# Delta rule's inverse: blocks of 32 by substitution in two passes, in place of blocks of 16 and one more doubling

## The chip, the cores and the metric

The kernel runs on one core of a Trainium2 chip. The core has TensorE (PE, matrix products and transposes), VectorE (DVE, elementwise work and sums along a row), ScalarE (ACT, activations and copies), GpSimd (POOL) and SyncE (SP, which issues most DMAs). The metric is the device time of one execution in microseconds (us); a time given for a kernel is the median of several executions.

## The reference, cut to what matters

One layer of a decoder trunk for 256 positions: a combined projection, three branches (gated delta rule, HGRN2, attention into a memory), their gated sum, an output projection and an MLP. The change is in the gated delta rule:

```python
def gated_deltanet(q, k, v, beta, logdecay):
    # chunkwise; per head and chunk
    dec = jnp.exp(jnp.where(causal, gam[..., :, None] - gam[..., None, :], -jnp.inf))
    lower = jnp.where(strict, bc[..., :, None] * jnp.einsum('bhnid,bhnjd->bhnij', kc, kc) * dec, 0.0)
    a_mat = lower + jnp.eye(CHUNK, dtype=lower.dtype)
    rhs = jnp.concatenate([vc * bc[..., None], kc * (bc * jnp.exp(gam))[..., None]], axis=-1)
    sol = lax.linalg.triangular_solve(a_mat, rhs, left_side=True, lower=True, unit_diagonal=True)
    ...
```

The kernel uses chunks of 128 positions in place of 64 and forms the inverse of the triangular matrix itself. There are 8 heads and two chunks; four heads make a head group, so one head group has 8 matrices of 128 x 128, and there are two head groups.

## The kernel before, in words

**Weights.** Most of the work is products of activations with f32 weights. A weight group is 256 rows by 512 columns of a weight matrix, 128 partitions x 1024 numbers in SBUF, 512 KB. SP loads it (`load_w_raw`, L163, tile w, four buffers); ACT casts it to a high part wh (L174); DVE takes the difference as a low part wl (L175); wh and wl have four buffers each. TensorE then makes three products of 512 columns per row block, or in the "joined" form two products of 512 and 256 columns (L206 to L208 in `unit`, L223 and L225 in `products_joined`). A unit has 8 such groups, or 4 in a branch's second projection.

**Background work.** Everything that is no weight product is written as Python generators, put in a list and advanced by `tick`, once per weight group. `rate` says how many generator steps (yields) one tick advances; R1 to R4 are its values in four stretches: R1 for the delta rule's projections, R2 for the units of branch C (attention's output), R3 for the projections of HGRN2, R4 for the units of branch A's output. The generators are taken first in, first out; a few short ones (convolution, gates) go ahead. The framework that builds the program then fixes the order on each engine's queue from these steps, its own estimates of durations, and the buffers that are free; at run time each engine takes its queue strictly in order.

**The inverse (`gen_a`, one per head group).** U holds the strictly upper part of eight matrices. Its diagonal blocks of BL = 16 go through DRAM: eight small writes into scr, and eight loads that give every one of the 16 rows of a block the whole block (tile Lb, 16 x 16 numbers for each of 8 matrices in each partition), both issued by POOL. DVE then does back substitution on all blocks at once, one column at a time (L880 multiplies, L881 sums, 15 columns), in Xc, a row of 16 numbers for each of the 8 matrices. L884 spreads Xc over the diagonal blocks of X with the block mask mblk. TensorE transposes X into XT (L891), and then doubles the block size from 16 to 32, from 32 to 64 (each: products pw L911 and pzt L916, a masked copy into XT L918, transposes back into X L924, copies L912 and L925) and from 64 to 128 (L900, L905). Behind that come the products with the values and the head norm. Xc and Lb have one buffer; tiles of the general pool (tag g) have 25.

**Masks.** `gen_masks` makes, early in the kernel and as background work, masks of diagonal blocks and mT[s], which marks the upper off-diagonal part that a doubling from s to 2s fills.

Of the kernel before, what the change touches and what calls it, by code (L numbers as in the profile page):

```python
# [10 lines left out]
F32 = mybir.dt.float32  # L11
# [3 lines left out]
ALU = mybir.AluOpType  # L15
AX = mybir.AxisListType

P = 128
D = 2048
S = 256  # L20
NT = S // P
# [12 lines left out]
KG = 2  # L34
BL = 16
WB = 4
R1, R2, R3, R4 = 1.1, 1.0, 1.0, 1.2


@with_exitstack  # L40
def tile_trunk(ctx: ExitStack, tc, a):
    nc = tc.nc
    V, A, T, G = nc.vector, nc.scalar, nc.tensor, nc.gpsimd

    cst = ctx.enter_context(tc.tile_pool(name="cst", bufs=1))
# [3 lines left out]
    lp = ctx.enter_context(tc.tile_pool(name="lp", bufs=1))  # L49
    sp = ctx.enter_context(tc.tile_pool(name="sp", bufs=16))  # L50
    sp64 = ctx.enter_context(tc.tile_pool(name="sp64", bufs=2))
    dp = ctx.enter_context(tc.tile_pool(name="dp", bufs=2, space=bass.MemoryType.DRAM))
# [5 lines left out]
    def nm(s):  # L58
        cnt[0] += 1
        return f"{s}_{cnt[0]}"  # L60

    def g4(name, shape=(P, 1024), dt=F32):
        return gp.tile(list(shape), dt, tag="g", name=nm(name))
# [11 lines left out]
    def bank(name):  # L75
        return pbp.tile([P, 512], F32, tag="bp", name=nm(name))

    def const(name, shape, dt=F32):
        return cst.tile(list(shape), dt, tag=name, name=name)
# [11 lines left out]
    pin = tc.keep_in_program_order  # L91
# [309 lines left out]
    mgtr = const("mgtr", [P, P], F32R)  # L401
    msk2 = const("msk2", [P, 2, P])
    dblk = const("dblk", [P, BL])
    mblk = const("mblk", [P, P])
    mT = {s: const(f"mT{s}", [P, P]) for s in (1, 2, 4, 8, 16, 32, 64)}

    def gen_masks():
        G.affine_select(out=mgt, in_=ones, pattern=[[-1, P]], base=0, channel_multiplier=1,
                        compare_op=ALU.is_gt, fill=0.0)
        G.affine_select(out=mlt, in_=ones, pattern=[[1, P]], base=0, channel_multiplier=-1,  # L410
                        compare_op=ALU.is_gt, fill=0.0)
        pin(V.tensor_tensor(out=caus, in0=mlt, in1=ident, op=ALU.add))
        pin(V.tensor_copy(mgtr, mgt))
        pin(V.tensor_copy(msk2[:, 0, :], mlt))
        pin(V.tensor_scalar(out=msk2[:, 1, :], in0=caus, scalar1=-1.0, scalar2=None, op0=ALU.mult))
        pin(V.tensor_reduce(out=dblk, in_=ident.rearrange("p (k c) -> p c k", c=BL), axis=AX.X, op=ALU.add))
        yield
        prev = ident
        for s in (1, 2, 4, 8, 16, 32, 64):
            b = 2 * s  # L420
            if b < P:
                cur = mblk if b == BL else cst.tile([P, P], F32, tag=f"blk{b.bit_length() % 2}", name=f"blk{b}")
                v3 = cur.rearrange("p (n s) -> p n s", s=b)
                G.affine_select(out=v3, in_=ones.rearrange("p (n s) -> p n s", s=b),
                                pattern=[[-b, P // b], [0, b]], base=0, channel_multiplier=1,
                                compare_op=ALU.is_ge, fill=0.0)
                G.affine_select(out=v3, in_=v3, pattern=[[b, P // b], [0, b]], base=b - 1,
                                channel_multiplier=-1, compare_op=ALU.is_ge, fill=0.0)
            else:
                cur = ones  # L430
            d = cst.tile([P, P], F32, tag="mdiff", name=f"mdiff{s}")
            pin(V.tensor_tensor(out=d, in0=cur, in1=prev, op=ALU.subtract))
            pin(V.tensor_tensor(out=mT[s], in0=d, in1=mlt, op=ALU.mult))
            prev = cur
            yield

# [138 lines left out]
    for u in range(2):  # L575
        k = unit_joined(lambda kt: memB[kt // 2][:, kt % 2], w_kv, 512 * u)
# [188 lines left out]
    def gen_a(hg, kc, qc, vc, z):  # L765
# [21 lines left out]
        for t in range(NT):  # L787
            dl = g4("dl", (P, 2, 4, P), F32R)
            pd = bank("dec")
            for i, l_ in enumerate((ldh, ldl)):  # L790
                V.tensor_tensor(out=dl[:, i], in0=bc(caus, 4),
                                in1=l_.bitcast(F32)[:, t, hs].unsqueeze(2).to_broadcast([P, 4, P]), op=ALU.mult)
# [5 lines left out]
        for t in range(NT):  # L798
            V.tensor_tensor(out=d2[t], in0=dec[:, t * 4:t * 4 + 4, :].unsqueeze(2).to_broadcast([P, 4, 2, P]),
                            in1=msk2.unsqueeze(1).to_broadcast([P, 4, 2, P]), op=ALU.mult)  # L800
# [13 lines left out]
        U, AQ = g4("U", (P, 8, P)), g4("AQ", (P, 8, P))  # L814
        rck = small("rck", 8)
        for t in range(NT):
            pks = [gram(t, t, hp) for hp in range(2)]
            for h in range(4):
                jk = g4("jk", (P, P))
                V.scalar_tensor_tensor(out=jk, in0=pks[h // 2][:, (h % 2) * S:(h % 2) * S + P], scalar=1.0, in1=ident,  # L820
                                       op0=ALU.mult, op1=ALU.mult, accum_out=sse[:, t * 4 + h:t * 4 + h + 1])
            ts = slice(t * 4, t * 4 + 4)
# [3 lines left out]
                                   op0=ALU.mult, op1=ALU.mult)  # L826
# [3 lines left out]
            for h in range(4):  # L830
                b = t * 4 + h
                for w, dst in ((0, U), (1, AQ)):
                    V.scalar_tensor_tensor(out=dst[:, b, :], in0=pks[h // 2][:, (h % 2) * S + w * P:(h % 2) * S + w * P + P],
                                           scalar=cneg[:, b:b + 1], in1=d2[t][:, h, w, :],
                                           op0=ALU.mult, op1=ALU.mult)
                if h % 2 == 1:
                    yield

        NB = P // BL
        scr = dp.tile([NB, 8, BL, BL], F32, tag="scr", name=nm("scr"))  # L840
        Lb = lp.tile([P, 8, BL * BL], F32, tag="lb", name=nm("lb"))
        for k in range(NB):
            sl = slice(k * BL, (k + 1) * BL)
            pin(G.dma_start(scr[k].rearrange("b c m -> c b m"), U[sl, :, sl]))
        for k in range(NB):
            G.dma_start(Lb[k * BL:(k + 1) * BL].rearrange("p b m -> p (b m)"),
                        scr[k:k + 1].rearrange("k b c m -> k (b c m)").to_broadcast([BL, 8 * BL * BL]))
        yield
        ct0, cp0 = small("ct0", 4), small("cp0", 4)
        V.tensor_tensor(out=ct0, in0=cneg[:, 0:4], in1=t0e[:, hs], op=ALU.mult)  # L850
# [11 lines left out]
        for t in range(NT):  # L862
# [3 lines left out]
            for h in range(4):  # L866
                b = t * 4 + h
# [2 lines left out]

        X, XT, W = g4("X", (P, 8, P)), g4("XT", (P, 8, P)), g4("W", (P, 8, P))
        V.memset(W, 0.0)
        V.memset(Lb[:, :, 0:BL * BL:BL + 1], 1.0)
        Xc = lp.tile([P, 8, BL], F32, tag="xc", name=nm("xc"))
        V.tensor_copy(Xc, dblk.unsqueeze(1).to_broadcast([P, 8, BL]))
        yield
        for c in range(BL - 2, -1, -1):
            n = BL - c
            tm = lp.tile([P, 8, BL], F32, tag="tm", name=nm("tm"), bufs=2)
            V.tensor_tensor(out=tm[:, :, 0:n], in0=Xc[:, :, c:BL], in1=Lb[:, :, c * BL + c:(c + 1) * BL], op=ALU.mult)  # L880
            V.tensor_reduce(out=Xc[:, :, c], in_=tm[:, :, 0:n], axis=AX.X, op=ALU.add)  # L881
            if c % 2 == 0:
                yield
        V.tensor_tensor(out=X.rearrange("p b (k c) -> p b k c", c=BL), in0=Xc.unsqueeze(2).to_broadcast([P, 8, NB, BL]),  # L884
                        in1=mblk.rearrange("p (k c) -> p k c", c=BL).unsqueeze(1).to_broadcast([P, 8, NB, BL]), op=ALU.mult)
        yield
        yield
        for t in range(NT):
# [2 lines left out]
                T.transpose(pt[:, h * P:(h + 1) * P], X[:, t * 4 + h, :], ident)  # L891
            A.copy(XT[:, t * 4:t * 4 + 4, :], pt.rearrange("p (h i) -> p h i", h=4))
        yield
        for s in (s_ for s_ in (2, 4, 8, 16, 32, 64) if s_ >= BL):
            last = s == 64
            pw = bank("pw")
            if last:

                for b in range(8):
                    T.matmul(pw[64:128, b * 64:(b + 1) * 64], U[0:64, b, 64:128], X[0:64, b, 0:64], start=True, stop=True)  # L900
                A.copy(W[64:128, :, 0:64], pw[64:128, :].rearrange("p (b s) -> p b s", b=8))
                yield
                pzt = bank("pzt")
                for b in range(8):
                    T.matmul(pzt[0:64, b * 64:(b + 1) * 64], W[64:128, b, 0:64], XT[64:128, b, 64:128],  # L905
                             start=True, stop=True)
                A.copy(XT[0:64, :, 64:128], pzt[0:64, :].rearrange("p (b s) -> p b s", b=8))
                yield
                break
            for b in range(8):  # L910
                T.matmul(pw[:, b * 64:(b + 1) * 64], U[:, b, :], half_view(X, s, False)[:, b], start=True, stop=True)  # L911
            A.copy(half_view(W, s, False), pw.rearrange("p (b n s) -> p b n s", b=8, s=s))  # L912
            yield
            pzt = bank("pzt")
            for b in range(8):
                T.matmul(pzt[:, b * 64:(b + 1) * 64], W[:, b, :], half_view(XT, s, True)[:, b],  # L916
                         start=True, stop=True)
            V.copy_predicated(half_view(XT, s, True), half_mask(mT[s], s, True),  # L918
                              pzt.rearrange("p (b n s) -> p b n s", b=8, s=s))
            yield  # L920
            for t in range(NT):
                pt = bank("X")
                for h in range(4):
                    T.transpose(pt[:, h * P:(h + 1) * P], XT[:, t * 4 + h, :], ident)  # L924
                A.copy(X[:, t * 4:t * 4 + 4, :], pt.rearrange("p (h i) -> p h i", h=4))  # L925
            yield
# [11 lines left out]
        for h in range(4):  # L938
            V.scalar_tensor_tensor(out=r1[:, h, :], in0=pr[:, h * P:(h + 1) * P],
                                   scalar=e1e[:, hg * 4 + h:hg * 4 + h + 1], in1=nv[:, 4 + h, :],  # L940
                                   op0=ALU.mult, op1=ALU.add)
# [236 lines left out]
    for hg in range(2):  # L1178
        k, g = forget(unit_joined(hboth, w_in, OFF_BF + 512 * hg), hg)
# [216 lines left out]
    for e in range(1, NE):  # L1396
        cur = mlp_in(e)
# [20 lines left out]
```

## Time and profile before

| | |
|---|---|
| median of 3 executions | 1807.99 us (1807.24 to 1808.0) |
| the profiled execution | 1807.64 us |
| its span, first to last instruction | 1805.9 us |
| DVE, L880 and L881, both head groups | 7.0 and 6.9 us, 30 instructions each |
| TensorE, busy in that span | 1794.3 us |

The span is what the views of the trace show; the rest of an execution's time lies around it. All times in the trace are counted from the span's start. The delta rule's inverses lie at about 357 to 421 us (head group 0) and 519 to 579 us (head group 1).

### The profile page before, as it was taken

What the parts mean: (1) busy time and instruction counts of PE and PEld (TensorE: products, weight loads), DVE (VectorE), ACT (ScalarE), POOL (GpSimd) and SP (SyncE); (2) the same over time, 40 slices, a digit from 0 to 9 for tenths busy, and PEclk for the clock granted to TensorE, in tenths of its full rate; (3) what the DMA queues carried; (4) which work ended last, traced back from release to release, by engine and by line L of the source; (5) the groups of instructions that cost most, each with busy time, mean ns of one, the idle gap of its engine ahead of it and who ended that gap; (6) DMA issues with size and microseconds to landing.
All of it is one profiled execution on the core that took longest, in us unless ns stands there. A gap on an engine that the chain in (4) does not pass through costs nothing.

```text
span 1805.9 us, 23842 instructions
## 1 busy us (share of the span) xinstructions
PE 1794.3 (99%) x9241; PEld 1531.7 (85%) x9241; DVE 1133.6 (63%) x1518; ACT 909.3 (50%) x1156; POOL 42.8 (2%) x68
## 2 busy tenths in 40 slices
PE   9999999999999999999999999999999999999998
PEld 7888888888888888888888888888888888888886
DVE  6865678755764677696555557655656565655556
ACT  7645565544564565555444445544444444444433
POOL 1000000200200000000000000000000000000000
PEclk9999999999999999999999999999999999999999
DMA  8575655754665556465666675566666666666664
GB/s 273 198 199 154 187 152 150 215 174 136 175 182 162 154 167 192 140 186 175 199 186 187 211 233 163 186 188 195 190 193 191 189 218 189 192 191 191 186 197 137
DMA packets 174946, 333.40 MB, mean 185 GB/s; under 512 B 13144, under 2 KB 14832, under 8 KB 174576
## 3 DMA queue, kind: packets, MB, share of 16 engines
q1 hardware_dynamic: 169280, 325.10, 58.7%
q10 hardware_dynamic: 4528, 4.54, 0.9%
q0 software_dynamic: 1024, 2.23, 0.7%
q8 instruction: 72, 1.18, 0.3%
q14 instruction: 42, 0.34, 0.1%
HBM read 329.60 MB, written 2.23 MB: 184 GB/s over the span
## 4 chain that ended last, share of the span: by engine, by line
PE 98%; issue 0%; DMA 0%; ACT 0%; DVE 0%; POOL 0%; DVEq 0%; POOLq 0%; ACTq 0%
PE mm L223 23%; PE mm L206 18%; PE mm L208 18%; PE mm L207 18%; PE mm L225 12%; PE pa L1115 1%; PE pw L911 0%; PE pzt L916 0%; DMA lrow<-in_lb_raw 0%; PE mm L367 0%; PE mm L368 0%; PE mm L370 0%; PE idle L331 0%; PE tr L1253 0%; PE tr L356 0%
## 5 line engine op out<-in xcount | busy, mean ns | idle before, releaser
L175 DVE TENSOR_TENSOR wl<-w,wh 128x1024 fp32r<-128x1024 f32 x600 | 731.1, 1223 | 519.2 <-ACT wh L174 517.5
L174 ACT CAST wh<-w 128x1024 fp32r<-128x1024 f32 x600 | 629.8, 1052 | 710.9 <-PE mm L208 445.1
L223 PE MATMUL mm<-h2h,wh 128*128 128x512 f32 x960 | 230.4, 391 | 0.0
L206 PE MATMUL mm<-wh,hh 128*128 128x512 f32 x576 | 227.5, 395 | 0.0
L208 PE MATMUL mm<-wh,hh 128*128 128x512 f32 x576 | 224.7, 390 | 0.0
L207 PE MATMUL mm<-wl,hh 128*128 128x512 f32 x576 | 224.4, 390 | 0.0
L223 PEld LDWEIGHTS mm<-h2h,wh 128*128 128x128 f32 x960 | 176.3, 188 | 34.1
L206 PE MATMUL mm<-wh,mh 128*128 128x512 f32 x512 | 199.2, 389 | 0.0
L207 PE MATMUL mm<-wl,mh 128*128 128x512 f32 x512 | 199.2, 389 | 0.0
L208 PE MATMUL mm<-wh,ml 128*128 128x512 f32 x512 | 199.2, 389 | 0.0
L223 PE MATMUL mm<-hh,wh 128*128 128x512 f32 x768 | 192.3, 393 | 0.3 <-DVE sum L261 0.3
L223 PEld LDWEIGHTS mm<-hh,wh 128*128 128x128 f32 x768 | 138.5, 189 | 25.8 <-issue 0.5
L208 PEld LDWEIGHTS mm<-wh,hh 128*128 128x128 f32 x576 | 108.1, 188 | 22.7
L225 PEld LDWEIGHTS mm<-h2h,wl 128*128 128x128 f32 x960 | 123.1, 191 | 4.7
L206 PEld LDWEIGHTS mm<-wh,hh 128*128 128x128 f32 x576 | 108.2, 188 | 21.4
L207 PEld LDWEIGHTS mm<-wl,hh 128*128 128x128 f32 x576 | 108.3, 188 | 21.2
L225 PE MATMUL mm<-h2h,wl 128*128 128x256 f32 x960 | 124.8, 283 | 0.0
L207 PEld LDWEIGHTS mm<-wl,mh 128*128 128x128 f32 x512 | 96.1, 188 | 20.0
L208 PEld LDWEIGHTS mm<-wh,ml 128*128 128x128 f32 x512 | 96.1, 188 | 19.9
L206 PEld LDWEIGHTS mm<-wh,mh 128*128 128x128 f32 x512 | 96.1, 188 | 19.9
L225 PEld LDWEIGHTS mm<-hh,wl 128*128 128x128 f32 x768 | 102.1, 191 | 5.7
L225 PE MATMUL mm<-hh,wl 128*128 128x256 f32 x768 | 104.9, 283 | 0.0
(388 smaller groups left out, 1919.2 us busy)
## 6 DMA issues: line engine op xcount, KB each, us to landing
w<-in_w_in SPq DMA_DIRECT2D x240, 512.0 KB, 3.8
w<-in_w_mlp_in SPq DMA_DIRECT2D x128, 512.0 KB, 3.9
w<-in_w_mlp_out SPq DMA_DIRECT2D x128, 512.0 KB, 3.9
w<-in_w_out SPq DMA_DIRECT2D x32, 512.0 KB, 4.2
w<-in_w_kv_mem SPq DMA_DIRECT2D x30, 512.0 KB, 5.1
w<-in_w_br_c SPq DMA_DIRECT2D x16, 512.0 KB, 4.2
w<-in_w_br_a SPq DMA_DIRECT2D x16, 512.0 KB, 4.5
w<-in_w_br_b SPq DMA_DIRECT2D x16, 512.0 KB, 3.6
```

The lines of the kernel that those rows point to most:

```text
L174: q(A.copy(wh[:, js, 0:width], w[:, js, 0:width]))
L175: q(V.tensor_tensor(out=wl[:, js, 0:width], in0=w[:, js, 0:width], in1=wh.bitcast(F32)[:, js, 0:width], op=ALU.subtract))
L206: T.matmul(o, st, wh[:, j, :], start=kt == 0, stop=False)
L207: T.matmul(o, st, wl[:, j, :], start=False, stop=False)
L208: T.matmul(o, sl, wh[:, j, :], start=False, stop=kt == nk - 1)
L223: T.matmul(ps[c], wh[:, j, c * P:(c + 1) * P], both[j], start=k0 + j == 0, stop=end)
L225: T.matmul(ps[c][:, 0:S], wl[:, j, c * P:(c + 1) * P], both[j][:, 0:S], start=False, stop=end)
L1115: T.matmul(pas[h][:, t * 192:t * 192 + 192], kp[:, h, t * P:(t + 1) * P], qp[:, h * 2 + t, 0:192], start=True, stop=True)
```

## The change

The substitution goes to blocks of 32 without a larger Lb. Each row of X keeps two halves of 16 columns in Xc (index w). First pass (w = 1): the substitution as before, each row with its own block of 16. Then, for the rows in the second half of a block of 32, the result is carried over to the first half's columns: the off-diagonal 16 x 16 blocks of U (written to scx and loaded into two tiles Lx of the general pool) are multiplied with the row and summed (the row product). Lb's rows of the second halves are loaded again with the first halves' blocks, and a second pass (w = 0) substitutes the first half's columns. rfirst and rsecond are columns of ones and zeros that tell the rows of the first half from those of the second. mblk becomes the mask of the diagonal blocks of 32 without their upper off-diagonal part. The doubling from 16 to 32 on TensorE is left out; those from 32 and 64 stay. R2 goes from 1.0 to 1.15 and R3 from 1.0 to 1.1.

```diff
-R1, R2, R3, R4 = 1.1, 1.0, 1.0, 1.2
+R1, R2, R3, R4 = 1.1, 1.15, 1.1, 1.2
...
+            if s == BL:
+                pin(V.tensor_tensor(out=mblk, in0=cur, in1=mT[s], op=ALU.subtract))
+                pin(V.tensor_reduce(out=rfirst, in_=mT[s], axis=AX.X, op=ALU.add))
+                pin(V.tensor_scalar(out=rfirst, in0=rfirst, scalar1=1.0 / BL, scalar2=None, op0=ALU.mult))
+                pin(V.tensor_scalar(out=rsecond, in0=rfirst, scalar1=-1.0, scalar2=1.0, op0=ALU.mult, op1=ALU.add))
...
+        scx = dp.tile([NB // 2, 8, BL, BL], F32, tag="scx", name=nm("scx"))
         Lb = lp.tile([P, 8, BL * BL], F32, tag="lb", name=nm("lb"))
+        Lx = [g4("Lx", (P, 4, BL * BL)) for t in range(NT)]
+
+        def spread(rows, src):
+            G.dma_start(rows, src.rearrange("k b c m -> k (b c m)").to_broadcast([rows.shape[0], rows.shape[1]]))
+
         for k in range(NB):
             sl = slice(k * BL, (k + 1) * BL)
             pin(G.dma_start(scr[k].rearrange("b c m -> c b m"), U[sl, :, sl]))
         for k in range(NB):
-            G.dma_start(Lb[k * BL:(k + 1) * BL].rearrange("p b m -> p (b m)"),
-                        scr[k:k + 1].rearrange("k b c m -> k (b c m)").to_broadcast([BL, 8 * BL * BL]))
+            spread(Lb[k * BL:(k + 1) * BL].rearrange("p b m -> p (b m)"), scr[k:k + 1])
+        for k in range(NB // 2):
+            r0 = 2 * k * BL
+            G.dma_start(scx[k].rearrange("b c m -> c b m"), U[r0:r0 + BL, :, r0 + BL:r0 + 2 * BL])
+        for k in range(NB // 2):
+            r0 = 2 * k * BL
+            for t in range(NT):
+                spread(Lx[t][r0:r0 + 2 * BL].rearrange("p b m -> p (b m)"), scx[k:k + 1, t * 4:t * 4 + 4])
...
-        V.memset(Lb[:, :, 0:BL * BL:BL + 1], 1.0)
-        Xc = lp.tile([P, 8, BL], F32, tag="xc", name=nm("xc"))
-        V.tensor_copy(Xc, dblk.unsqueeze(1).to_broadcast([P, 8, BL]))
-        yield
-        for c in range(BL - 2, -1, -1):
...
+        Xc = lp.tile([P, 8, 2, BL], F32, tag="xc", name=nm("xc"))
+        V.tensor_copy(Xc[:, :, 1, :], dblk.unsqueeze(1).to_broadcast([P, 8, BL]))
+        yield
+
+        def substitute(w):
+            V.memset(Lb[:, :, 0:BL * BL:BL + 1], 1.0)
+            for c in range(BL - 2, -1, -1):
+                n = BL - c
+                tm = lp.tile([P, 8, BL], F32, tag="tm", name=nm("tm"), bufs=2)
+                V.tensor_tensor(out=tm[:, :, 0:n], in0=Xc[:, :, w, c:BL], in1=Lb[:, :, c * BL + c:(c + 1) * BL],
+                                op=ALU.mult)
+                V.tensor_reduce(out=Xc[:, :, w, c], in_=tm[:, :, 0:n], axis=AX.X, op=ALU.add)
+                if c % 2 == 0:
+                    yield
+
+        yield from substitute(1)
+
+        for k in range(NB // 2):
+            spread(Lb[(2 * k + 1) * BL:(2 * k + 2) * BL].rearrange("p b m -> p (b m)"), scr[2 * k:2 * k + 1])
+        V.tensor_scalar(out=Xc[:, :, 0, :], in0=Xc[:, :, 1, :], scalar1=rsecond, scalar2=None, op0=ALU.mult)
+        for t in range(NT):
+            ts = slice(t * 4, t * 4 + 4)
+            lx = Lx[t].rearrange("p b (c m) -> p b c m", c=BL)
+            V.tensor_tensor(out=lx, in0=Xc[:, ts, 0, :].unsqueeze(2).to_broadcast([P, 4, BL, BL]), in1=lx, op=ALU.mult)
+            yield
+            V.tensor_reduce(out=Xc[:, ts, 0, :], in_=lx, axis=AX.X, op=ALU.add)
+            yield
+        yield from substitute(0)
+        V.scalar_tensor_tensor(out=Xc[:, :, 0, :], in0=Xc[:, :, 1, :], scalar=rfirst, in1=Xc[:, :, 0, :],
+                               op0=ALU.mult, op1=ALU.add)
...
-        for s in (s_ for s_ in (2, 4, 8, 16, 32, 64) if s_ >= BL):
+        for s in (s_ for s_ in (2, 4, 8, 16, 32, 64) if s_ >= 2 * BL):
```

More of the change, by code (lines that the diff above doesn't have):

```diff
@@ L404, in tile_trunk @@
     mblk = const("mblk", [P, P])
+    rfirst, rsecond = const("rfirst", [P, 1]), const("rsecond", [P, 1])
     mT = {s: const(f"mT{s}", [P, P]) for s in (1, 2, 4, 8, 16, 32, 64)}
@@ L421, in gen_masks @@
             if b < P:
-                cur = mblk if b == BL else cst.tile([P, P], F32, tag=f"blk{b.bit_length() % 2}", name=f"blk{b}")
+                cur = cst.tile([P, P], F32, tag=f"blk{b.bit_length() % 2}", name=f"blk{b}")
                 v3 = cur.rearrange("p (n s) -> p n s", s=b)
@@ L872, in gen_a @@
         V.memset(W, 0.0)
-        V.memset(Lb[:, :, 0:BL * BL:BL + 1], 1.0)
-        Xc = lp.tile([P, 8, BL], F32, tag="xc", name=nm("xc"))
-        V.tensor_copy(Xc, dblk.unsqueeze(1).to_broadcast([P, 8, BL]))
+        Xc = lp.tile([P, 8, 2, BL], F32, tag="xc", name=nm("xc"))
+        V.tensor_copy(Xc[:, :, 1, :], dblk.unsqueeze(1).to_broadcast([P, 8, BL]))
         yield
-        for c in range(BL - 2, -1, -1):
[L878 to L882, printed above, removed]
-                yield
@@ L884, in gen_a @@
-        V.tensor_tensor(out=X.rearrange("p b (k c) -> p b k c", c=BL), in0=Xc.unsqueeze(2).to_broadcast([P, 8, NB, BL]),
-                        in1=mblk.rearrange("p (k c) -> p k c", c=BL).unsqueeze(1).to_broadcast([P, 8, NB, BL]), op=ALU.mult)
+        def substitute(w):
[8 more added lines that the diff above has]
+                    yield
@@ new lines, in gen_a @@
+        yield from substitute(0)
+        V.scalar_tensor_tensor(out=Xc[:, :, 0, :], in0=Xc[:, :, 1, :], scalar=rfirst, in1=Xc[:, :, 0, :],
+                               op0=ALU.mult, op1=ALU.add)
+        V.tensor_tensor(out=X.rearrange("p b (k c) -> p b k c", c=2 * BL),
+                        in0=Xc.rearrange("p b w c -> p b (w c)").unsqueeze(2).to_broadcast([P, 8, NB // 2, 2 * BL]),
+                        in1=mblk.rearrange("p (k c) -> p k c", c=2 * BL).unsqueeze(1).to_broadcast([P, 8, NB // 2, 2 * BL]),
+                        op=ALU.mult)
```

## The prediction

> **What bounds the kernel now.** I read the page first (busy shares, slices, chain), then the waits of TensorE alone, then the order of time on PE around the code that goes.
>
> ```profile
> PE 1794.3 (99%) x9241; PEld 1531.7 (85%) x9241; DVE 1133.6 (63%) x1518; ACT 909.3 (50%) x1156; POOL 42.8 (2%) x68
> ...
> PE   9999999999999999999999999999999999999998
> ...
> PEclk9999999999999999999999999999999999999999
> ...
> PE 98%; issue 0%; DMA 0%; ACT 0%; DVE 0%; POOL 0%; DVEq 0%; POOLq 0%; ACTq 0%
> ```
>
> ```profile
> PE idle L331 <- POOL ident L84: 1.6, 1, 1.6
> PE dec L793 <- DVE dl L791: 1.0, 1, 1.0
> ```
>
> The chain that ended last is 98% TensorE, TensorE is full in every slice, the granted clock does not fall, and its two longest waits for another engine are 1.6 and 1.0 us, one at the start and one in the delta rule's decay, which the change leaves alone. So what is worth something is what TensorE no longer has to issue. A busy share of 99% does not say how long one product holds the engine, since products overlap; for that I take start-to-start times. These are PE's rows for the first doubling of head group 0, with an undisturbed stretch of 12 products (one weight group) ahead of it:
>
> ```profile
> 361.02 0.39 PE L206 MATMUL mm<-wh,hh 128*128 128x512 f32 x1
> ...
> 363.74 0.39 PE L206 MATMUL mm<-wh,hh 128*128 128x512 f32 x1
> ...
> 389.80 1.89 PE L911 MATMUL pw<-X,U 128*128 128x64 f32 x16
> 391.50 0.48 PE L206 MATMUL mm<-wh,hh 128*128 128x512 f32 x1
> ...
> 394.35 1.89 PE L916 MATMUL pzt<-XT,W 128*128 128x64 f32 x16
> ...
> 398.87 1.04 PE L924 MATMUL X<-ident,XT 128*128 128x128 f32 x8
> 399.67 0.47 PE L206 MATMUL mm<-wh,hh 128*128 128x512 f32 x1
> ...
> 402.51 1.89 PE L911 MATMUL pw<-X,U 128*128 128x64 f32 x16
> ```
>
> A weight group takes 363.74 - 361.02 = 2.72 us. One such group lies between each two of the doubling's three parts.
>
> **What goes.** From the start of pw to the start of pzt are 4.55 us, of which the weight group is 2.72: the first product costs 1.83. From pzt to the transposes 4.52, so 1.80; from the transposes to the next doubling 3.64, so 0.92. Together **4.55 us** for head group 0. The parts alone (389.80 to 391.50, 398.87 to 399.67) are 1.70 and 0.80; the other 0.1 or so per part is lost when PE changes over. Head group 1 has the same three parts, inside the f unit of branch B:
>
> ```profile
> 547.69 1.90 PE L911 MATMUL pw<-X,U 128*128 128x64 f32 x16
> 549.39 1.20 PE L225 MATMUL mm<-hh,wl 128*128 128x256 f32 x8
> ...
> 552.27 1.89 PE L916 MATMUL pzt<-XT,W 128*128 128x64 f32 x16
> 553.98 1.17 PE L223 MATMUL mm<-hh,wh 128*128 128x512 f32 x4
> ...
> 556.86 1.04 PE L924 MATMUL X<-ident,XT 128*128 128x128 f32 x8
> 557.65 1.17 PE L223 MATMUL mm<-hh,wh 128*128 128x512 f32 x4
> ```
>
> 1.70 + 1.71 + 0.79 = 4.20 us, and with changeovers between nothing and head group 0's 0.35, 4.2 to 4.55; I take 4.45. Sum: **9.0 us**, with ends at 8.4 (no changeover in either) and 9.1. Nothing is added to TensorE. The copies on ACT (L912, L925) go too; ACT is half idle and I give that no value.
>
> **What comes.** On DVE, by these groups (both head groups together; mean ns of one; the idle time before them last):
>
> ```profile
> L175 DVE TENSOR_TENSOR wl<-w,wh 128x1024 fp32r<-128x1024 f32 x600 | 731.1, 1223 | 519.2 <-ACT wh L174 517.5 <-PE pT L632 0.9
> L880 DVE TENSOR_TENSOR tm<-xc,lb 128x16 f32<-128x16 f32 (+14 forms) x30 | 7.0, 234 | 0.9
> L881 DVE TENSOR_REDUCE xc<-tm 128x8 f32<-128x16 f32 (+14 forms) x30 | 6.9, 230 | 0.9
> L884 DVE TENSOR_TENSOR X<-xc,mblk 128x1024 f32<-128x1024 f32 x2 | 2.4, 1223 | 0.0
> L739 DVE TENSOR_REDUCE ss<-sq 128x8 f32<-128x1024 f32 x4 | 4.9, 1218 | 4.0 <-ACT sq L737 4.0
> L833 DVE SCALAR_TENSOR_TENSOR U<-kk,cneg,d 128x128 f32<-128x128 f32 x16 | 5.5, 345 | 0.1
> L918 DVE COPY_PREDICATED XT<-mT,pzt 128x512 f32<-128x512 int32 x4 | 2.9, 728 | 16.0 <-PE pzt L916 16.0
> ```
>
> The second pass of the substitution repeats L880 and L881: 3.5 + 3.45 us per head group and 0.9 between them, 7.85. The row product is two multiplications and two sums over 1024 elements a partition: 2 x 1.22 + 2 x 1.22 = 4.9, by L884 (which has broadcast operands too) and L739; the new sum leaves 64 results instead of 8, and I find no row that makes that dearer. Three small ones (masking, combining, the second memset) at 0.35 at most each by L833, less one L918 (0.73), leave 0.3. That is **13.05 us of DVE per head group**. The masks get four small instructions more at the start, 4 x 0.35 at most, beside weight units. Has DVE the room?
>
> ```profile
> 300.00:325.00 25.00, 25.00 (x152) 22.37 (x151) 22.51 (x62) 12.36 (x16) 2.06 (x1) 1.00 0.58 180
> 350.00:425.00 75.00, 75.00 (x405) 63.41 (x404) 38.62 (x61) 35.88 (x46) 0.00 (x0) 1.00 0.54 159
> 515.00:590.00 75.00, 75.00 (x466) 65.89 (x465) 41.44 (x67) 39.23 (x49) 0.00 (x0) 1.00 0.52 154
> ```
>
> (Columns: stretch, its length, then busy time of PE, weight loads, DVE, ACT, POOL; clock, DMA share, GB/s.) In the 75 us around each inverse DVE works 38.6 and 41.4 us; with 13.05 more, 52 and 54, or 69 to 73%. In 300 to 325 it works 90% and PE still has 25.00 of 25.00. Densest is the row product: at 1.15 steps a tick a weight group of 2.72 us brings one split of 1.22 and 1.15 x 1.22 of row product, 2.63 us or 97%; the substitution, 8 steps of about 1 us, makes 88%. Up to four split weight groups (the pool has four buffers) stand ready ahead of PE, 10.9 us, so an overshoot of 1 or 2 us is covered: cost 0. Without that cover it would be those 1 or 2 us per head group.
>
> The rest costs TensorE nothing by itself. The chain to the inverse gets longer by the DVE work and the reload of lb, less the doubling's own stretch (389.80 to 402.51, 12.7 us); the inverse of a head group has only the branch output to serve, and the other head group or branch fills PE. Steps: 12 more yields (8 second substitution, 4 row product) less 3, so 9 per head group, 18 in all. The new rates give 48 x 0.15 + 64 x 0.10 = 13.6 more; the 4.4 left move into the last stretch, where the drain after branch 0's units issues at most a few of them at once, ahead of a gate unit of 8 groups (21.8 us) that needs none of it: 0.
>
> On POOL and the DMA queues there are, per head group, 4 small writes (scx), 8 loads of Lx (32 rows x 4 KB, 128 KB each) and 4 reloads of lb, 128 KB each: 1.05 + 0.52 MB beside the 1.05 MB of lb today. POOL issues them at about 0.48 us each (row of L846 below, 3.85 us for 8), some 8 us a head group, and is 2% busy. The reload waits for the last read of the first pass; behind it in POOL's queue stands only the power for this head group's own norm, which comes after the inverse.
>
> **Rivals.** First, **the weights run short while Lx loads**. Below: queues over 335 to 340 us, when lb of head group 0 lands (q0 is POOL's queue, q1 the weights'), and ACT just after it.
>
> ```profile
> q0 software_dynamic: 164, 0.61, 69.2%
> q1 hardware_dynamic: 143, 0.29, 28.2%
> ```
>
> ```profile
> 342.63 1.05 ACT L174 CAST wh<-w 128x1024 fp32r<-128x1024 f32 x1 [2.74 <-DMA w<-in_w_in]
> ```
>
> The weights got 0.29 MB in 5 us, and PE uses 0.524 MB every 2.72 us. Lx, 1.05 MB at 0.61 MB per 5 us, would hold that on for 8.6 us: 0.50 MB arrive, 1.66 are used, 1.16 MB or 6.0 us of PE are missing. After lb alone ACT already waited 2.74 us for a weight, so the raw buffers were empty and only the split ones, 10.9 us when full, are left. Against a stall: PE showed none here. For it: 6.0 us out of a lead that is no longer full. I price it at 0 to 5 us, 3 likely, once: 1802. [...]
>
> Second, the slower side: **TensorE stands at the transposes of X** (L891), which lie in its queue at a place fixed in advance, with all weight products behind them.
>
> ```profile
> 531.00 1.23 DVE L884 TENSOR_TENSOR X<-xc,mblk 128x1024 f32<-128x1024 f32 x1
> ```
>
> ```profile
> 532.88 1.04 PE L891 MATMUL XT<-ident,X 128*128 128x128 f32 x8
> ```
>
> ```profile
> 330.19 3.85 POOL L846 DMA_DIRECT2D lb<-scr  x8
> ```
>
> ```profile
> 357.23 0.17 DVE L873 MEMSET lb<- 128x128 f32 x1
> ```
>
> ```profile
> DMA to landing us min/median/max: 4.5/7.9/9.6
> ```
>
> In head group 1 only 0.65 us lie between the end of X (532.23) and L891. With a reload in the chain, any delay beyond what the order allows for is PE's. The reload takes 4 x 0.49 + 9.6 = 11.5 us at its longest today; the row product (5 us, about 9 with the splits between) covers most. If landing doubled behind Lx, some 12 us would be missing in each group: 24 - 9 = 15 us slower, 1823. It decides at 4.5 us a group (the gain is gone) and at 6.3 (slower by 0.2%). Against it: the order leaves DMAs much room, since L873 runs 357.23 - 334.04 = 23 us after the last issue of lb, where 9.6 is the longest landing.
>
> A third, that DVE's extra 26 us become the bound, needs more than 10.9 us of backlog; by the shares above it gives at most the 1 or 2 us a group, 1801 to 1803, and I count it with the first.
>
> **Numbers.** The profiled execution took 1807.64 us (span 1805.9 and 1.7 around it), 0.35 under the median of 1807.99. 1807.64 - 9.0 = 1798.6; against the median **1799.0**. Chances: forecast, 1797.3 to 1801, 0.64; weights short or DVE dense, to 1804.4, 0.14; late X with part or all of the gain lost, 0.13; late X beyond it, 0.09. 0.2% (3.6 us) is what a measurement of this kernel can tell from no change, so faster 0.78, same 0.13, slower 0.09. The range 1797.3 to 1806 reaches into the late X and leaves out just under 0.2.
>
> **What would show it.** Right: no L911/L916/L924 rows of the first doubling, weight groups at 2.72 us where they were, PE's waits for others still near 3 us in all, L880 and L881 at x60. Rival one: PE idle between 340 and 360 us ended by wl, with ACT waiting for w. Rival two: PE idle at L891 ended by DVE X, and DVE idle at the second memset ended by lb. Wrong altogether: PE's weight products spaced wider than 0.227 us, or a doubling's PE rows still there.

## The result and the profile after

The changed kernel takes **1828.26 us** (median of 4, 1827.7 to 1828.96) against 1807.99 (1807.24 to 1808.09): 20.3 us slower, ratio 1.0114 with a 95% interval of 1.0102 to 1.0126. The forecast was 1799.0. The execution that the views of after show has a span of 1826.8 us, 20.9 more than before.

From the page of the changed kernel: busy shares, the slices of PE and of its clock, the chain that ended last.

```profile
PE 1791.6 (98%) x9161; PEld 1526.4 (84%) x9161; DVE 1156.0 (63%) x1594; ACT 904.3 (49%) x1148; POOL 59.0 (3%) x100
...
PE   9999999699989999999999999999999999999998
...
PEclk9999999899999999999999999999999999999999
...
PE 92%; issue 3%; DMA 2%; DVE 2%; POOL 1%; ACT 0%; SPq 0%; DVEq 0%; POOLq 0%; ACTq 0%
```

TensorE issues 80 instructions fewer, as it should, but two slices are no longer full (the 8th, at 320 to 365 us, and the 12th, from 502 us), the clock falls in the first of them, and 6% of the chain left TensorE. The waits of TensorE for other engines (total, times, longest) say where:

```profile
PE mm L206 <- DVE sum L261: 16.2, 1, 16.2
PE mm L223 <- ACT sg L1041: 4.5, 1, 4.5
PE mm L223 <- DVE mg L1045: 2.7, 1, 2.7
PE idle L331 <- POOL ident L84: 1.6, 1, 1.6
PE dec L800 <- DVE dl L798: 0.9, 1, 0.9
```

(Line numbers are those of the kernel that a view shows.) The last two were there before; the first three, 23.4 us, are new. None is at the transposes of X, none is for a weight. (A row of the views below gives start and length in us; in brackets stand the idle time of its engine just before it and what, by the view, ended it.)

**The first stall** lies in head group 0. DVE's queue in order of time, then PE's:

```profile
330.84 1.22 DVE L175 TENSOR_TENSOR wl<-w,wh 128x1024 fp32r<-128x1024 f32 x1 [0.66 <-ACT wh L174]
344.56 0.17 DVE L899 MEMSET lb<- 128x128 f32 x1 [12.50 <-DMA scx<-U]
...
347.39 1.28 DVE L261 TENSOR_TENSOR sum<-mm,sum 128x512 f32<-128x512 f32 x2
```

```profile
330.98 1.04 PE L885 MATMUL vT<-ident,cv 128*128 128x128 f32 x8
348.22 0.76 PE L206 MATMUL mm<-wh,hh 128*128 128x512 f32 x1 [16.20 <-DVE sum L261]
```

L899 is the memset of the first pass, which writes the ones into lb's diagonals and so must wait until lb has been loaded; L261 is the addition that takes finished products out of PSUM, here those of av1, the value projection of head group 1. The memset stands ahead of L261 in the queue. It waits 12.50 us for transfers (the view names the DMA that came last by its records; the memset itself writes only lb), six columns of the substitution follow, and only then L261. PSUM has two buffers for such products (pmm, bufs=2), both are held, so TensorE cannot begin the next unit. In the kernel before, the same part of DVE's queue was:

```profile
327.39 0.69 DVE L261 TENSOR_TENSOR sum<-mm,sum 128x512 f32<-128x512 f32 x1 [0.89 <-ACT sum L260]
...
330.31 0.68 DVE L261 TENSOR_TENSOR sum<-mm,sum 128x512 f32<-128x512 f32 x1
```

There the memset came at 357.23, 27 us behind the second L261. The instructions on DVE did not get longer; two of them changed places.

**The second stall** lies in head group 1. DVE, then PE:

```profile
527.71 0.17 DVE L899 MEMSET lb<- 128x128 f32 x1
527.91 0.17 DVE L903 TENSOR_TENSOR tm<-xc,lb 128x16 f32<-128x16 f32 x1
...
535.90 1.16 DVE L1045 TENSOR_TENSOR mg<-mm,sg 128x1024 f32<-128x1024 f32 x1
```

```profile
529.82 2.07 PE L223 MATMUL mm<-hh,wh 128*128 128x512 f32 x4 [4.50 <-ACT sg L1041]
531.69 1.77 PE L225 MATMUL mm<-hh,wl 128*128 128x256 f32 x8
533.29 1.08 PE L223 MATMUL mm<-hh,wh 128*128 128x512 f32 x4
537.12 2.07 PE L223 MATMUL mm<-hh,wh 128*128 128x512 f32 x4 [2.75 <-DVE mg L1045]
539.00 1.54 PE L225 MATMUL mm<-hh,wl 128*128 128x256 f32 x8
540.38 2.89 PE L223 MATMUL mm<-hh,wh 128*128 128x512 f32 x12
```

Here the memset waits for nothing, but nearly the whole first pass (527.91 to 535) stands ahead of L1045, another instruction that empties PSUM. ACT's evacuation into sg has moved back too:

```profile
528.74 1.02 ACT L1041 ACTIVATE sg<-mm 128x1024 f32<-128x1024 f32 x1
```

Its unit's last product starts at 511.68. Ahead of sg in ACT's queue stand casts of later weight groups, the last at 525.36, and four activations of the delta rule (L879, 526.31 to 527.45). In the kernel with the order mended (e5 below) the same step runs at 496.86, 3.8 us after the last product (493.05), where here it is 17.1 us.

**What a stall costs beyond itself** is in the granted clock. Windows of the changed kernel just behind the first stall (length, then busy time of PE, weight loads, DVE, ACT, POOL; granted clock, DMA share, GB/s):

```profile
348.00:352.00 4.00, 3.78 (x9) 3.04 (x10) 4.00 (x11) 3.89 (x14) 1.17 (x3) 0.50 0.72 174
352.00:356.00 4.00, 4.00 (x18) 3.25 (x18) 3.80 (x8) 4.00 (x11) 0.00 (x0) 0.97 0.00 0
```

At a clock of 0.50, nine products take the place of 18: some 1.8 us lost. Behind the two waits in head group 1, one L223 x4 and one L225 x8 take 533.29 - 529.82 = 3.47 and 540.38 - 537.12 = 3.26 us; ahead of the stalls such a pair takes 329.56 - 327.68 = 1.88 (below), so 3.0 us are lost in both.

```profile
327.68 1.12 PE L225 MATMUL mm<-hh,wl 128*128 128x256 f32 x8
328.63 1.09 PE L223 MATMUL mm<-hh,wh 128*128 128x512 f32 x4
329.56 0.28 PE L606 MATMUL kk<-kqh 128*128 128x256 f32 x1
```

The account: waits 23.4, slow clock 1.8 + 3.0, together 28.2 us. Without them the changed kernel would take 1828.3 - 28.2 = 1800.1, close to the forecast. The experiments test whether that is so, and what in the change puts the memset there.

### The profile page after: what moved, and what is told of

It reads as the page before. It is cut to its first block, busy times and chain, and to the rows that moved or that the text cites. A ratio compares the mean times of both kernels' runs of the same rounds, so it can differ in the third digit from the quotient of the medians.

```text
span 1826.8 us, 23802 instructions
## 1 busy us (share of the span) xinstructions
PE 1791.6 (98%) x9161; PEld 1526.4 (84%) x9161; DVE 1156.0 (63%) x1594; ACT 904.3 (49%) x1148; POOL 59.0 (3%) x100
## 4 chain that ended last, share of the span: by engine, by line
PE 92%; issue 3%; DMA 2%; DVE 2%; POOL 1%; ACT 0%; SPq 0%; DVEq 0%; POOLq 0%; ACTq 0%
PE mm L223 22%; PE mm L206 17%; PE mm L208 17%; PE mm L207 17%; PE mm L225 12%; PE pa L1157 1%; DMA lb<-scr 1%; DMA scx<-U 1%; POOL scr L858 0%; DMA w<-in_w_kv_mem 0%; POOL nr L836 0%; PE mm L368 0%; PE mm L370 0%; PE mm L367 0%; DMA w<-in_w_in 0%
## 5 line engine op out<-in xcount | busy, mean ns | idle before, releaser
L206 PE MATMUL mm<-wh,hh 128*128 128x512 f32 x576 | 227.8, 395 | 16.2 <-DVE sum L261 16.2
L223 PE MATMUL mm<-h2h,wh 128*128 128x512 f32 x960 | 230.4, 391 | 0.0
L223 PEld LDWEIGHTS mm<-h2h,wh 128*128 128x128 f32 x960 | 176.4, 188 | 34.1
L223 PE MATMUL mm<-hh,wh 128*128 128x512 f32 x768 | 193.7, 396 | 7.5 <-ACT sg L1041 4.5
L223 PEld LDWEIGHTS mm<-hh,wh 128*128 128x128 f32 x768 | 139.4, 190 | 34.1 <-ACT sg L1041 4.9
L225 PEld LDWEIGHTS mm<-h2h,wl 128*128 128x128 f32 x960 | 123.1, 191 | 4.7
L225 PE MATMUL mm<-h2h,wl 128*128 128x256 f32 x960 | 124.8, 283 | 0.0
L225 PEld LDWEIGHTS mm<-hh,wl 128*128 128x128 f32 x768 | 103.4, 193 | 6.0
L225 PE MATMUL mm<-hh,wl 128*128 128x256 f32 x768 | 106.1, 285 | 0.0
```

The costliest lines, as they stand in the source:

```text
L206: T.matmul(o, st, wh[:, j, :], start=kt == 0, stop=False)
L223: T.matmul(ps[c], wh[:, j, c * P:(c + 1) * P], both[j], start=k0 + j == 0, stop=end)
L225: T.matmul(ps[c][:, 0:S], wl[:, j, c * P:(c + 1) * P], both[j][:, 0:S], start=False, stop=end)
```

## The experiments

Four theories. **Q**: the order of DVE's queue; the rest of the change does what it should. **T**: the additional transfers (Lx, scx, the second load of lb) hold something up, and the order is only where it shows. **W**: 13 us more DVE work per head group are too much. **S**: the 18 more steps, the new rates or the longer chain. Each time stands against runs of the kernel before on the same chip (1807.11, 1807.16 and 1807.33 in the three groups, e1 to e4, e5 to e8, e9).

### e1: the memset held in place

```diff
         def substitute(w):
-            V.memset(Lb[:, :, 0:BL * BL:BL + 1], 1.0)
+            q = pin if w else (lambda i: i)
+            q(V.memset(Lb[:, :, 0:BL * BL:BL + 1], 1.0))
```

> The changed kernel with one thing undone: the first pass's memset of the diagonals is held, in DVE's queue, behind what the program writes ahead of it (av1's two evacuations of PSUM among it). Same transfers, same tiles, same DVE work, same steps. Theory Q (the order of DVE's queue: a memset that waits 12.5 us for its data stands ahead of an evacuation that TensorE needs): the 16.2 us wait of PE for sum and the 1.8 us of slow products behind it go, 18.0 in all, and head group 1, whose order the edit leaves alone, keeps its 7.2 us of waits and some 3 us of slow clock: 1828.3 - 18.0 = 1810 (1808 to 1813). Rival T (the transfers of Lx starve TensorE or fall behind, and the order is only where this shows): PE waits as long for another thing between 330 and 360, wl or XT, and the time stays at 1825 to 1829. Rival W (13 us more DVE work per head group is too much): DVE keeps its work, so 1825 to 1829 too.

`pin` holds an instruction, in its engine's queue, behind what the program writes ahead of it. Measured: 1810.86 us, ratio 1.0018 (1.0009 to 1.0028), so 17.4 us less than the changed kernel. TensorE's waits, and L261 at the place of the first stall:

```profile
PE mm L223 <- ACT sg L1042: 4.5, 1, 4.5
PE mm L223 <- DVE mg L1046: 1.9, 1, 1.9
...
PE mm L206 <- DVE sum L261: 0.8, 1, 0.8
```

```profile
330.97 1.28 DVE L261 TENSOR_TENSOR sum<-mm,sum 128x512 f32<-128x512 f32 x2
```

L261 runs where it did, TensorE waits 0.8 us for it instead of 16.2, and nothing comes in its place. The transfers, the tiles and the DVE work are all still there: T and W are out for head group 0. Head group 1 keeps its stall. e1 lies 11.3 us over e5 below: 7.2 us are the three waits, and some 4 us the slow clock behind those of head group 1 (0.50 for 5 us from 511.5 on, 0.53 for 3.5 us from 520 on).

### e2: no loads of Lx

```diff
-        for k in range(NB // 2):
-            r0 = 2 * k * BL
-            for t in range(NT):
-                spread(Lx[t][r0:r0 + 2 * BL].rearrange("p b m -> p (b m)"), scx[k:k + 1, t * 4:t * 4 + 4])
+        for t in range(NT):
+            G.memset(Lx[t], 0.0)
```

> The changed kernel with the 8 loads of Lx per head group left out (two memsets fill Lx, so the row product is made with zeros); scx is still written, and both passes, the row product, the tiles and all steps stay. Theory Q: in this kernel both head groups' evacuations stand ahead of the memset, so all stalls go: 1828.3 - 28.2 = 1800 (1798 to 1803), PE's waits near 3 us. Rival T says the same here (1798 to 1803). Rival W, and a rival S (the 18 more steps and the new rates, or the longer chain): the work and the steps are all there, so the time stays above 1820.

Measured: 1799.31 us, ratio 0.9957 (0.9942 to 0.9972). All waits of TensorE are back at 1.7 us and less. Both passes, the row product (with zeros in Lx), all steps and the new rates run in this kernel, and the tiles Lx are taken where the changed kernel takes them: W and S are out, and so are the tiles by themselves. The memset of head group 0 is back behind the evacuations (326.91 and 329.82):

```profile
356.71 0.17 DVE L897 MEMSET lb<- 128x128 f32 x1
```

So the loads of Lx are what moves it. Between Q and T this run can't choose; e1 and e5 do.

### e3: no second pass

```diff
-        yield from substitute(0)
```

> The changed kernel without the second pass of the substitution (the row product's sums are taken as the second block): 7.85 us of DVE and 8 steps less per head group; transfers stay, and in head group 0 the memset still stands ahead of av1's evacuations. Theory Q and rival T: stall 1 stays, 16 us of wait and 1.8 of slow clock; head group 1 has the memset ahead of one mg evacuation, a wait of 0 to 7 us: 1817 to 1829. Rival W: 15.7 us of the 26.1 us of added DVE work are gone, so most of the 20.3 us should be: 1800 to 1813.

Measured: 1823.51 us, ratio 1.0092 (1.0077 to 1.0107), inside Q's range; W's 1800 to 1813 is missed by 10 us though 15.7 us of DVE work are gone. TensorE's waits:

```profile
PE mm L206 <- DVE sum L261: 14.5, 1, 14.5
PE mm L206 <- DVE tm L903: 6.1, 1, 6.1
```

The first stall is there as in the changed kernel. The second, 6.1 us, has the size that was given, but is put down to another instruction of the substitution, not to mg. By the times it is mg: TensorE starts again at 518.57, just after this row ends (518.43).

```profile
517.21 1.22 DVE L1044 TENSOR_TENSOR mg<-mm,sg 128x1024 f32<-128x1024 f32 x1
```

### e4: the kernel before, with lb loaded twice

```diff
         for k in range(NB):
             G.dma_start(Lb[k * BL:(k + 1) * BL].rearrange("p b m -> p (b m)"),
                         scr[k:k + 1].rearrange("k b c m -> k (b c m)").to_broadcast([BL, 8 * BL * BL]))
+        for k in range(NB):
+            G.dma_start(Lb[k * BL:(k + 1) * BL].rearrange("p b m -> p (b m)"),
+                        scr[k:k + 1].rearrange("k b c m -> k (b c m)").to_broadcast([BL, 8 * BL * BL]))
```

> The kernel before, with one thing added: the 8 loads of lb are issued twice in a row (1.05 MB more per head group, as much as the loads of Lx). The doubling, the steps, the rates and the DVE work are those of before. In head group 1 the order of DVE's queue comes out with the memset and the whole substitution ahead of two evacuations of PSUM; in head group 0 it does not. Theory Q: no stall at 330 to 390, and in head group 1 a PE wait for sum of 4 to 14 us and 1 to 3 us of slow clock behind it: 1808 + 5 to 17 = 1813 to 1825. Rival T: waits for wl or lb in both head groups, of equal size. Rivals W and S: nothing of them is in here, 1807 to 1810.

Measured: 1828.11 us (four executions, 1821.62 to 1829.12), ratio 1.0109 (1.0091 to 1.0126). So 1.05 MB more of loads per head group cost the old kernel, with none of the new arithmetic, as much as the whole change. That is more than the 5 to 17 us given, and the wait is another one:

```profile
PE XT L894 <- DVE X L887: 12.3, 2, 11.9
PE mm L223 <- DVE mg L1006: 2.4, 1, 2.4
...
PE mm L206 <- ACT wh L174: 1.2, 1, 1.2
...
PE mm L207 <- DVE wl L175: 0.8, 1, 0.8
```

```profile
541.09 0.17 DVE L876 MEMSET lb<- 128x128 f32 x1
...
549.29 1.23 DVE L887 TENSOR_TENSOR X<-xc,mblk 128x1024 f32<-128x1024 f32 x1
550.43 1.28 DVE L261 TENSOR_TENSOR sum<-mm,sum 128x512 f32<-128x512 f32 x2
```

```profile
550.57 1.97 PE L894 MATMUL XT<-ident,X 128*128 128x128 f32 x8 [11.88 <-DVE X L887]
```

The block of memset, substitution and X stands ahead of two evacuations, as said; but TensorE's own place for the transposes of X comes first, so it stood there, as in the prediction's second rival. The memset did not wait for lb here either; the block as a whole comes late for TensorE. The waits for wh and wl, 2.0 us in head group 0, are of the first rival's kind (T): these two waits are what can be put down to the additional bytes themselves. Q gives the main part and its place, T a small part.

### e5: Lx loaded later

```diff
-        Lx = [g4("Lx", (P, 4, BL * BL)) for t in range(NT)]
...
-        for k in range(NB // 2):
-            r0 = 2 * k * BL
-            for t in range(NT):
-                spread(Lx[t][r0:r0 + 2 * BL].rearrange("p b m -> p (b m)"), scx[k:k + 1, t * 4:t * 4 + 4])
...
-        yield from substitute(1)
+        for i, _ in enumerate(substitute(1)):
+            if i == 3:
+                Lx = [g4("Lx", (P, 4, BL * BL)) for t in range(NT)]
+                for k in range(NB // 2):
+                    r0 = 2 * k * BL
+                    for t in range(NT):
+                        spread(Lx[t][r0:r0 + 2 * BL].rearrange("p b m -> p (b m)"), scx[k:k + 1, t * 4:t * 4 + 4])
+            yield
```

> The changed kernel, whole, with the two tiles Lx taken and loaded four steps into the first pass instead of right behind the loads of lb. Same bytes, same DVE work, same steps and rates. Theory Q: with this the memset stands behind the evacuations in both head groups, so no stall is left and the 9.0 us of the first doubling remain: 1799 (1797.5 to 1801.5), PE's waits near 3 us, and nothing waits at the row product for Lx longer than DVE's own slack hides. Rival T (the transfers cost TensorE time wherever they run): 1.05 MB per head group still land beside the weights, so 1803 to 1815. Rival W or S: 1815 or more.

Measured: **1799.58 us** (1799.29 to 1799.76), ratio 0.9958 (0.9944 to 0.9971). This is the change whole, and it beats both kernels. TensorE's waits, all but those under 0.9 us:

```profile
PE idle L331 <- POOL ident L84: 1.6, 1, 1.6
PE dec L800 <- DVE dl L798: 0.9, 1, 0.9
```

One pair of rows says more than the time. POOL in the changed kernel, then in e5, then DVE in e5:

```profile
345.26 3.91 POOL L854 DMA_DIRECT2D Lx<-scx  x8 [5.73 <-DMA scx<-U]
```

```profile
343.42 3.95 POOL L853 DMA_DIRECT2D Lx<-scx  x8 [4.67 <-DMA w<-in_w_in]
```

```profile
357.06 0.17 DVE L894 MEMSET lb<- 128x128 f32 x1
```

On the chip the loads that were written later are issued 1.8 us earlier: POOL's queue has the same order in both kernels, the loads of Lx right behind the writes of scx. What the edit moved is the place of the memset, from 344.56 (ahead of the evacuations) to 357.06. So the transfers of Lx did not hold up TensorE; their place in the program changed an order that was fixed before anything ran.

### e6: no tiles Lx, scx loaded into lb

```diff
         for k in range(NB // 2):
-            spread(Lb[(2 * k + 1) * BL:(2 * k + 2) * BL].rearrange("p b m -> p (b m)"), scr[2 * k:2 * k + 1])
+            r0 = 2 * k * BL
+            spread(Lb[r0:r0 + 2 * BL].rearrange("p b m -> p (b m)"), scx[k:k + 1])
...
-            lx = Lx[t].rearrange("p b (c m) -> p b c m", c=BL)
+            lx = Lb[:, ts, :].rearrange("p b (c m) -> p b c m", c=BL)
...
+        for k in range(NB):
+            spread(Lb[k * BL:(k + 1) * BL].rearrange("p b m -> p (b m)"), scr[k - k % 2:k - k % 2 + 1])
         yield from substitute(0)
```

> The changed kernel, whole, without tiles Lx: when the first pass is done, scx is loaded into lb itself, and after the row product lb is loaded again in full (12 loads instead of 8 + 4, each waiting for DVE's last read). The chain to X gets longer by one wait for transfers in each head group; the burst behind lb is gone. Theory Q: the evacuations stand ahead of the memset in both head groups, so 1799 (1797.5 to 1801.5), unless TensorE's places for XT come before X is there. Rival X (the longer chain reaches TensorE at XT, rival two of the prediction): PE waits at the transposes of X for DVE X, 3 us or more in a head group: 1802 to 1815.

Measured: 1817.57 us, ratio 1.0062 (1.0049 to 1.0074). Q's 1799 is missed, and the rival X given with it holds, with 2.6 us more than its upper end. TensorE's waits:

```profile
PE XT L931 <- DVE X L922: 7.0, 2, 6.3
PE mm L206 <- ACT sg L1039: 2.1, 1, 2.1
PE mm L206 <- DVE sum L261: 1.9, 1, 1.9
PE oT L767 <- DVE on L758: 1.8, 1, 1.8
```

The first pass is in its good place, and the second pass, behind one more load, is late for TensorE's place for XT. The four waits are 12.8 us of the 18.0 that e6 lies over e5; behind the 6.3 us wait the clock is 0.50 from 427.31 to 435.31, which is 4.0 us of work lost. The last 1.2 us were not taken apart.

### e7 and e8: one step instead of four; the old rates

e7 is e5 with `i == 0` for `i == 3`. e8 is the changed kernel with

```diff
-R1, R2, R3, R4 = 1.1, 1.15, 1.1, 1.2
+R1, R2, R3, R4 = 1.1, 1.0, 1.0, 1.2
```

> As the kernel with Lx loaded later, but one step into the first pass instead of four. In head group 0 the order is the good one; in head group 1 the memset and five columns of the substitution stand ahead of the evacuation into mg. Theory Q: nothing at 330 to 350; in head group 1 PE waits for mg by what the memset waits for lb, and no longer than 7 us, with up to 3 us of slow clock behind it: 1799 to 1809. Rival T: the same as four steps in, to 1 us.

> The changed kernel with the old rates (R2 and R3 back at 1.0). In head group 0 the order is that of the changed kernel; in head group 1 the memset and 12 columns of the first pass stand ahead of two evacuations of sum, and no split of weights lies between them. Theory Q: the 18.0 us of head group 0 stay, and head group 1 has waits for sum or wl of 3 to 12 us instead of 7.2: 1820 to 1834. Rival S (the new rates are the cause): back to 1798 to 1810.

e7: 1801.31 us, ratio 0.9967 (0.9955 to 0.9979). Within Q's range, at its lower end and 1.7 us over e5; TensorE's new waits there are 1.7 us for sum and 0.4 for mg, so the five columns ahead of the evacuation into mg cost next to nothing; the memset there did not wait for lb. T's "the same to 1 us" fails by 0.7, no strong test. e8: 1831.07 us, ratio 1.0132 (1.0118 to 1.0146), inside Q's range. Its waits:

```profile
PE mm L206 <- DVE sum L261: 15.5, 1, 15.5
PE mm L223 <- DVE sum L261: 10.9, 2, 10.6
```

Both stalls are there without the new rates. S is out for the rates as well.

### e9: e5 with the old rates

> The whole changed kernel with Lx loaded four steps into the first pass, and the old rates (R2 and R3 at 1.0). The evacuations stand ahead of the memset in both head groups. Prediction's step on the steps (18 more yields against 13.6 more from the rates, the rest drained behind a gate unit at no cost): if steps left over cost nothing, the 18 that are now left over cost nothing either, and the time is that of the same kernel with the new rates, 1799.6 within 2 us. Rival S: the drain issues 18 steps in a lump that TensorE must wait for, 3 to 10 us more.

Measured: 1801.52 us, ratio 0.9969 (0.9956 to 0.9981): 1.9 us over e5, within the 2 that were given. The one new wait is that of the head norm's transposes (oT, L767), 1.7 us as in e8. So the 13.6 steps that the new rates add are worth some 1.7 us, and no lump of steps stands at the end.

## Why the prediction was wrong, by its own steps

**What bounds the kernel, and what goes: right, a little too large.** With the order mended, the change gives 7.6 us by medians (1807.16 - 1799.58) and 7.9 by the spans of the profiled executions (1805.9 - 1798.0), where 9.0 was forecast and 8.4 was the lower end. Counted over the whole trace from each product's start to the next start, TensorE spends 3.27 us less on pw, 3.40 on pzt and 1.58 on the transposes in e5 than before, 8.25 together, close to the 8.4 of the bare rows. The 0.6 added for changeovers (9.0 - 8.4) did not come back: the weight products, where they would show, take 1681.4 us in e5 and 1681.3 before. What else lies between 8.25 and 7.9 is under 0.4 us in each row and was not taken apart.

**What comes on DVE: right in size, and free.** In e5 the row product's instructions took 1.218 and 1.210 us (1.22 forecast), and the two passes 60 instructions of 234 and 60 of 228 ns as against 234 and 230. TensorE waited for none of them. The cover by split weights held as well: TensorE's waits name neither wl nor wh in the changed kernel or in e5.

**The failed step is "The rest costs TensorE nothing by itself"**, with the paragraph on POOL and the DMA queues behind it. It priced the new transfers by what they would do on the chip, bytes, POOL's time and queue, and there it was nearly right: e5 makes all of them and is 0.3 us over e2, which makes none of the loads of Lx. It left out that a transfer's place in the program is an input to the order of the queues, and took the order of before for that of after. The sentence against the second rival shows it: "the order leaves DMAs much room, since L873 runs 357.23 - 334.04 = 23 us after the last issue of lb". Those 23 us were no property of the kernel but the result of one arrangement. In the changed kernel the memset comes 344.56 - 334.20 = 10.4 us after the last issue of lb (POOL's row of 330.35, 3.85 us long), about when lb has landed (the longest of these eight landings took 10.6 us), with two evacuations of PSUM behind it. The prediction asked what is queued behind the reload on POOL; it did not ask it of the memset on DVE, which is the first instruction to wait for lb and was queued among the evacuations.

**Rivals.** The first, weights short, did not come in the changed kernel (2.0 us of that kind in e4). The second, late X at XT, did not come there either, but is real: 6.3 us in e6, 11.9 in e4. The slower side that did come was named by neither: the memset of the *first* pass, not the second, and PSUM, not XT, as what TensorE lacked. So the chance of 0.09 for slower rested on the wrong mechanism, and the range ended 22 us short.

**The steps and the rates:** "the 4.4 left move into the last stretch ... 0" agrees with e5, and e9 bounds it: with all 18 left over the price is 1.7 to 1.9 us.

**What stays open.** Why the framework orders the memset so when Lx's loads are written ahead of the first pass: its estimates leave no trace. What is shown is which edits do it (loads of Lx there, in the changed kernel, e3 and e8, and in head group 1 of e1; lb twice, in e4 for head group 1; loads one step into the pass, in e7 for five columns in head group 1) and which don't (no loads, e2; loads four steps into the pass, e5). That its own time for transfers makes TensorE late in its plan would fit all of them; this was argued, not measured.

## What to carry to other kernels

Where a framework fixes each engine's queue ahead of the run, a profile of before gives the price of work but not its place: after any edit that adds a transfer, read each in-order queue for an instruction that waits on a DMA, or a long block of other work, that stands ahead of one that empties PSUM (here a memset that waited 12.50 us on DVE, and 16.2 us lost on TensorE). It is worth trying to write a load nearer to its consumer than to its source: in e5 it started no later on the chip (343.42 against 345.26), and the order around it stayed. There is a limit: e6 loaded so late that X was late for TensorE, by 6.3 us at the longest. When a kernel gets slower by more than any of its added work could cost, look first for two instructions that changed places.

## What was not expected of the hardware

The granted clock halved behind a pause far shorter than the long stall: TensorE waited 2.75 us ahead of 537.12, and this is the window from there on in the changed kernel, with a clock of 0.50:

```profile
537.00:539.00 2.00, 1.88 (x5) 1.49 (x6) 1.11 (x5) 0.00 (x0) 1.14 (x3) 0.50 0.03 8
```

After 16.2 us of pause the products came 0.427 us apart (348.78, 349.21, 349.64) up to 352.20, 4.0 us behind the first at 348.22, and about 0.23 apart from then on. The 2.75 us pause was followed by a clock of 0.50 too; a wait of 4.5 us had ended only 4.6 us before it. The length of a pause alone did not decide it: in e1 a wait of 1.87 us ahead of 518.82, with one of 4.5 us shortly before it too, was followed by a clock of 0.53 from 520 to 523.5, and in e4 a wait of 2.41 us ahead of 518.90, with no other near it, by a full clock (1.00 from 500 to 525). Nor was the price fixed. Behind the three waits of the changed kernel it was 1.4 to 1.8 us each, behind the 6.3 us wait of e6 it was 4.0. What decides whether the clock falls, and for how long, no run shows.
